# The final norm's factor row, made on TensorE instead of through DRAM, in a decoder layer's kernel

## The chip, the cores and the metric

One core of a Trainium2 chip runs the kernel. The metric is the device time in microseconds (us) of one execution. The core's engines work side by side, each through its own list of instructions in order: TensorE (PE, with its weight loads as PEld), VectorE (DVE), ScalarE (ACT), GpSimd (POOL) and SyncE (SP), which here issues the DMAs.

## The reference, cut to what matters

One layer of a hybrid decoder over 2048 prompt tokens and 8 sample tokens, 2056 in all, width 1024, float32:

```python
def _rmsnorm(x, g):
    return x * lax.rsqrt(jnp.mean(x * x, axis=-1, keepdims=True) + EPS) * g

def _layer(...):
    xr, gr, q, k, v = jnp.split(_rmsnorm(x, norm1_g) @ w_in, IN_SPLITS, axis=-1)
    rec = recurrence(conv(xr)) * gelu(gr)         # RG-LRU branch
    att = sliding_window_attention(q, k, v, sinks)
    mix = concatenate([_rmsnorm(rec, rec_norm_g), _rmsnorm(att, attn_norm_g)])
    h = x + mix @ w_out
    hn = _rmsnorm(h, norm2_g)
    return h + (silu(hn @ w_gate) * (hn @ w_up)) @ w_down     # D_FF = 2816

y = _rmsnorm(_layer(...), final_norm_g)           # the final norm
```

The change concerns the last line: each token's y (1024 values) is multiplied by one factor of that token, 1/sqrt(mean of squares + EPS), and by the gain of the feature.

## The kernel before

Activations lie transposed: features on the 128 partitions, tokens along the free dimension, so 1024 features are 8 tiles (m = 0 to 7). A factor that belongs to a token must therefore stand in every partition of a row, as a tile of 128 x tokens.

The first 600 us or so take the tokens in four blocks through the norm, the input projection, recurrence, attention and output projection; the sum h goes to DRAM (hs). Then comes the feed-forward part, in three groups of tokens (gi = 0, 1, 2) of two halves each (n = 0, 1): 2 x 344 tokens in group 0, 2 x 342 in groups 1 and 2. For each of 11 pairs p of D_FF chunks, a Strassen-like scheme makes seven products r of the gate side (ps_g) and of the up side (ps_u) in `products`, and seven of the down side (pw, for group and pair "pw1_0" is group 1, pair 0) in `down_parts`; each product is three TensorE matmuls of 342 or 344 columns, of split operands. VectorE adds every pw product into the y tiles of its group (L2175). `y_load` (L1893) fetches h into these y tiles by DMA (y<-hs, L1899), 16 tiles for each group, in buffers which the group before gives free when its y is stored.

At a group's end comes the final norm. Groups 0 and 1 go through `finish` (L2177), group 2 through `finish_last`. `finish` sums the squares of a half's eight y tiles, `rstd_cols` (L1119) sums over partitions by matmuls (st_f) and raises to the power -1/2, which gives the factors as columns: w tokens on the partitions, nt columns (w, nt = 86, 4 in group 0; 114, 3 in group 1). `dram_bcast` (L1152) turns these columns into a row: TensorE transposes them (tr_f, L1075), ScalarE copies the result out of PSUM (row_f, L1149), SyncE writes it to a row in DRAM (rows_f, L1150) and reads it back into all 128 partitions (rb_f, L1156). Then VectorE multiplies each y tile by gain and factor (L2195) and SyncE stores it (out_yT, L2196).

`row_bcast` (L1128) does the same without DRAM: for each column one matmul, with the column broadcast along its free dimension as weights and the identity as the moving operand, leaves the w factors in all partitions of a PSUM bank (bc), and ScalarE copies the bank into the row tile (L1140). The first part of the kernel uses it for its norms (bc_at, bc_rc, bc_x); `finish_last` has such products (bc_f) of its own.

The work is written as generators that run by planned due times (`Chains`); the engines' lists are then put in a fixed order by `order_engines`, from the table ORDER, which has one long string for each engine. A word such as `tr_f1_1` names a generator or a group of matmuls; `:3` means three in a row, `+2` the third of those left. SyncE, ScalarE, GpSimd and VectorE each work through their own string; a DMA's issue on SyncE waits until what it reads is written, and what stands behind it in the list waits too.

Of the kernel before, what the change touches and what calls it, by code (L numbers as in the profile page):

```python
# [155 lines left out]
pt5_0_0 op0_1_0 op0_0_0 op0_0_260:2 op0_0_0:3 op0_0_260 op0_0_0 op0_1_0 op0_0_260:2 op0_0_0 op0_0_260 op0_0_0
op0_0_260 op0_0_0 op0_1_0 op0_0_260:2 op0_1_0:5 o4_1_0:2 op0_1_260:7 o4_1_1:2 op0_1_260:14 op0_2_0 op0_1_260 op0_2_0
pt5_0_1 op0_1_260 pt5_0_1 op0_1_260 pt5_0_1 op0_2_0:3 pt5_0_1 op0_2_0:14 op0_2_260 op0_2_0 op0_2_260 op0_2_0:2
op0_2_260 op0_2_0 op0_3_0 o5_0_0 op0_2_260:2 op0_2_0 op0_2_260:2 s6_1_0 op0_2_260:2 o5_0_0 s6_1_0:2 op0_2_260:2 s6_1_0
s6_1_1:2 op0_2_260 s6_1_1 op0_2_260:2 s6_1_1 op0_2_260:10 op0_3_0:4 o5_0_1 op0_3_0:16 pt5_1_0 op0_3_0 pt5_1_0 op0_3_0  # L160
op0_3_260:2 op0_3_0 op0_3_260 pt5_1_0:2 op0_3_260 o5_0_1 op0_3_260:9 g1_2_0_0 op0_3_260 g1_2_0_0 op0_3_260:8 op0_4_0
g1_2_0_0 op0_3_260 op0_4_0:6 op0_3_260 op0_4_0:10 g1_2_1_0:2 op0_4_0:4 g1_2_1_0 op0_4_0 op0_4_260 op0_4_0 op0_4_260:3
op0_4_0 op0_4_260:17 pt5_1_1 op0_4_260:3 pt5_1_1:2 op0_5_0:2 pt5_1_1 op0_5_0:2 o5_1_0 op0_5_0 o5_1_0 op0_5_0:13
op0_5_260 op0_5_0:4 o5_1_1 op0_5_260:2 op0_5_0 op0_5_260 op0_5_0 op0_5_260:8 s7_0_0:2 op0_5_260:2 s7_0_0:2 s7_0_1:2
op0_5_260 pt6_0_0 op0_5_260 pt6_0_0 op0_5_260:3 pt6_0_0:2 op0_5_260 o5_1_1 op0_6_0 op0_5_260:3 s7_0_1:2 op0_5_260
# [796 lines left out]
def hybrid_step(tc, xT, xR, vecs, cst, gatew, win, wout, wgate, wup, wdown, kT, vC, ck, cv, sconv, sh0,  # L962
# [5 lines left out]
    with ExitStack() as ctx:  # L968
# [183 lines left out]
        def dram_bcast(cols, w, nt, name):  # L1152
            row = dp.tile([1, w * nt], F32, name=f"rows_{name}")
            rows_out(row, cols, w, nt, name)
            out = bcp.tile([P, TM], F32, tag="bc", name=f"rb_{name}")
            nc.sync.dma_start(out[:, :w * nt], row.to_broadcast([P, w * nt]))  # L1156
            return out
# [1226 lines left out]
```

## Time and profile before

| | us |
|---|---|
| runs shown | 1998.69, 1999.23, 3230.68; median 1999.23 |
| profiled execution | 1999.11 |
| its span (first to last instruction) | 1997.0 |
| TensorE busy in the span | 1971.0 |
| VectorE, ScalarE, GpSimd busy | 1560.6, 981.3, 959.8 |

The span is what the views of the profile cover; 2.1 us of the profiled time lie around it. Times in the views are counted from the start of the span. Granted TensorE clock is 0.997. Group 0's end, in the sense of this text, is about 1120 to 1165 us, group 1's about 1570 to 1615.

A row of a timeline reads: start, duration, engine, line and operation, output<-inputs, tile shapes, and in brackets the idle time ahead of it with what ended it. A row of a list of waits reads: engine and operation, what it waited for, then total, number of times and longest. Where a row of a window has four engines in a row, the first number is the window's length, the others the busy time of PE, PEld, DVE, ACT and POOL with the number of instructions.

### The profile page before, as it was taken

The numbers are of one execution on the slowest core, as the hardware profiler recorded it, in microseconds if no ns is written. First come the engines' busy times: TensorE is split into PE (matmuls) and PEld (weight loads), VectorE is DVE, ScalarE is ACT, GpSimd is POOL, SyncE is SP. The second block draws the span as 40 slices with busy tenths as digits, with TensorE's granted clock in tenths as the row PEclk, the third lists the DMA queues.
The fourth block names the chain that finished last, engine by engine and source line by source line (L and its number), as shares of the span: only waits on it lengthen the run. The fifth ranks groups of instructions, "written<-read, shape, count | busy, mean of one in ns | idle before, by whom it ended". The sixth has DMA issues, their size and how long they took to land. (4 is left out here: it accounts for less than half of the span.)

```text
span 1997.0 us, 34846 instructions
## 1 busy us (share of the span) xinstructions
PE 1971.0 (99%) x12112; PEld 1874.8 (94%) x12112; DVE 1560.6 (78%) x2894; ACT 981.3 (49%) x2032; POOL 959.8 (48%) x821
## 2 busy tenths in 40 slices
PE   8999999999999999999999999999999999999998
PEld 8988898888877999999999999999999999999998
DVE  7887986777986888888998786886668586766776
ACT  6775774664664534444446433433345433433433
POOL 5412362130233896788998754534456423322323
PEclk9999999999999999999999999999999999999999
DMA  8873586576688978655667886776558675565552
GB/s 314 287 252 138 194 300 198 183 254 210 223 283 291 335 263 268 220 215 210 246 241 279 265 289 231 234 237 210 191 191 267 228 259 199 179 211 195 180 181 103
DMA packets 218470, 461.93 MB, mean 231 GB/s; under 512 B 26230, under 2 KB 90406, under 8 KB 218278
## 3 DMA queue, kind: packets, MB, share of 16 engines
q1 hardware_dynamic: 214662, 456.69, 67.4%
q10 hardware_dynamic: 3632, 3.02, 0.4%
q8 instruction: 95, 1.56, 0.3%
q14 instruction: 81, 0.66, 0.1%
HBM read 345.51 MB, written 115.17 MB: 231 GB/s over the span
## 5 line engine op out<-in xcount | busy, mean ns | idle before, releaser
L1070 PE MATMUL ps_g<-hn,w_g 128*128 128x342 f32 (+1 forms) x2772 | 569.4, 320 | 0.3 <-DMA w_g<-split_g 0.3
L1070 PE MATMUL ps_u<-hn,w_u 128*128 128x342 f32 (+1 forms) x2772 | 559.5, 320 | 1.5 <-DMA w_u<-split_u 0.9
L1070 PEld LDWEIGHTS ps_g<-hn,w_g 128*128 128x128 f32 x2772 | 461.3, 188 | 1.2 <-ACT wd L1972 0.5
L1070 PEld LDWEIGHTS ps_u<-hn,w_u 128*128 128x128 f32 x2772 | 459.5, 188 | 3.0 <-ACT c_u L2115 1.6
L2175 DVE TENSOR_TENSOR y<-y,pw 128x342 f32<-128x342 f32 (+1 forms) x756 | 359.1, 504 | 114.7 <-PE pw L1070 108.4
L1070 PE MATMUL ip<-xn,w_in 128*128 128x512 f32 (+1 forms) x1680 | 365.2, 357 | 6.1 <-ACT xn L1105 5.7
L1070 PEld LDWEIGHTS ip<-xn,w_in 128*128 128x128 f32 x1680 | 269.6, 189 | 45.8 <-ACT xn L1105 5.7
L1070 PE MATMUL pw<-fh,wd 128*128 128x342 f32 (+1 forms) x864 | 253.4, 320 | 0.5 <-DVE y L2175 0.5
L1070 PE MATMUL pw<-t,wd 128*128 128x342 f32 (+1 forms) x972 | 243.7, 320 | 2.8 <-DVE y L2175 2.7
L1070 PE MATMUL op<-mix,w_out 128*128 128x512 f32 (+1 forms) x960 | 205.8, 355 | 0.4 <-ACT mix L1544 0.4
L1070 PEld LDWEIGHTS op<-mix,w_out 128*128 128x128 f32 x960 | 157.5, 189 | 25.3 <-ACT mix L1544 0.8
L1070 PEld LDWEIGHTS pw<-t,wd 128*128 128x128 f32 x972 | 169.9, 188 | 4.9 <-DVE y L2175 4.0
L1973 POOL TENSOR_TENSOR wd<-rd,wd 128x512 fp32r<-128x512 f32 x85 | 121.8, 1434 | 103.4 <-ACT wd L1972 99.1
L1972 ACT CAST wd<-rd 128x512 fp32r<-128x512 f32 x159 | 98.6, 621 | 130.0 <-PE ps_u L1070 39.8
L1070 PEld LDWEIGHTS pw<-fh,wd 128*128 128x128 f32 x864 | 158.6, 188 | 1.2 <-DVE y L2175 0.8
L1904 POOL TENSOR_TENSOR w_u<-ru,w_u 128x512 fp32r<-128x512 f32 x44 | 61.4, 1395 | 170.2 <-ACT w_u L1903 95.9
L1070 PE MATMUL pw<-fl,wd 128*128 128x342 f32 (+1 forms) x432 | 132.9, 320 | 0.0
L2089 DVE TENSOR_TENSOR c_u<-c_u,ps_u 128x342 f32<-128x342 f32 (+1 forms) x99 | 50.2, 508 | 101.2 <-PE ps_u L1070 93.9
L2071 POOL TENSOR_TENSOR c_u<-c_u,c_g 128x342 f32<-128x342 f32 (+1 forms) x60 | 65.4, 1090 | 124.8 <-DVE c_u L2089 115.1
L2060 DVE TENSOR_TENSOR fl<-c_u,fh 128x342 fp32r<-128x342 f32 (+1 forms) x132 | 105.4, 803 | 17.7 <-ACT fh L2059 17.0
L2059 ACT CAST fh<-c_u 128x342 fp32r<-128x342 f32 (+1 forms) x132 | 63.0, 480 | 110.6 <-POOL c_u L2071 49.3
L1070 PE MATMUL pd<-fh,w_d 128*128 128x344 f32 (+1 forms) x384 | 92.9, 320 | 0.0
(319 smaller groups left out, 3490.7 us busy)
## 6 DMA issues: line engine op xcount, KB each, us to landing
w_g<-split_g SPq DMA_DIRECT2D x88, 512.0 KB
w_u<-split_u SPq DMA_DIRECT2D x88, 512.0 KB
w_in<-split_w SPq DMA_DIRECT2D x84, 512.0 KB
rg<-in_wgate SPq DMA_DIRECT2D x110, 256.0 KB
ru<-in_wup SPq DMA_DIRECT2D x110, 256.0 KB
w_out<-split_w SPq DMA_DIRECT2D x48, 512.0 KB
split_g<-w_g SPq DMA_DIRECT2D x44, 512.0 KB
split_u<-w_u SPq DMA_DIRECT2D x44, 512.0 KB
```

The costliest lines, as they stand in the source:

```text
L1070: r = nc.tensor.matmul(*args, **kw)
L1904: lo_eng.tensor_tensor(w[:, 1, :], src, w[:, 0, :].bitcast(F32), op=ALU.subtract)
L1972: nc.scalar.copy(w[:, :, 0], v)
L1973: eng((E_DLO0, E_DLO1, E_DLO2)[gi][j]).tensor_tensor(w[:, :, 1], v, w[:, :, 0].bitcast(F32), op=ALU.subtract)
L2059: nc.scalar.copy(hi, v)
L2060: nc.vector.tensor_tensor(lo, v, hi.bitcast(F32), ALU.subtract)
L2071: (nc.vector if p == NPAIR - 1 or src is not v else eng(E_MUL[2 * h + n])).tensor_tensor(v, src, g, op=ALU.mult)
L2089: nc.vector.tensor_tensor(o, a, b, op)
L2175: nc.vector.tensor_tensor(v, v, ps, ALU.add)
```

## The change

In `finish` the factor row is made by `row_bcast` instead of `dram_bcast`. For each half of groups 0 and 1 that removes a transpose, a copy of 4 x 86 or 3 x 114, a DMA into DRAM and a broadcast DMA out of it, and adds 4 or 3 matmuls (bc_f) and a copy of 128 x 344 or 128 x 342. The multiplies and the stores are as before.

```diff
@@ -2188,7 +2190,7 @@
                 rstd_cols(acc[:, :nn], w, nt, 0, cols[:w, :nt], name, 0)
                 yield t + dt * (F_FIN[2] + F_FIN[3])
-                bc = dram_bcast(cols[:w, :nt], w, nt, name)
+                bc = row_bcast(cols[:w, :nt], w, nt, name, 0)
                 for m in range(KD):
                     yield t + dt * (F_FIN[2] + F_FIN[3])
                     v = ys[gi, n, m]
```

All five strings of ORDER are new, with the counts of all other instructions as they were. Two lines of the string of SP and of PE, before and after, from the same places (the end of group 1):

```diff
-wd2.0:2 wg2.1:4 wd2.0 wg2.2 wd2.0:2 wu2.1+4 wd2.1 f11 wu2.1 f11 wg2.2 wd2.1 wu2.1+1 wu2.1 f11+7 f10 f11+2 wu2.1 f11+4
+wd2.0:2 wu2.1+4 wd2.1 wu2.1 wg2.2 wd2.1 wu2.1+1 wu2.1 f11+5 f11+2 f11+4 f11+4 f11+1 f11+2 wu2.1 f10+2 f10+5 f10+5
```

What stands in the lists now is shown at three places. First TensorE at the end of group 0. Before, the second half's transpose (tr_f0_0) stands among the first pw products of group 1 (shape out, then the number of equal rows):

```order
L1070 MATMUL pw1_0_1_1_13737<-fl1_0_00_7464,wd1_0_0_13581 128x342
L1070 MATMUL pw1_0_5_1_13747<-fh1_0_01_7461,wd1_0_0_13581 128x342
L1070 MATMUL pw1_0_5_0_13742<-fh1_0_01_7461,wd1_0_0_13581 128x342
L1075 MATMUL tr_f0_0_13640<-cs_104,cols_f0_0_13538 4x86
L1070 MATMUL pw1_0_5_1_13747<-fl1_0_01_7465,wd1_0_0_13581 128x342
L1070 MATMUL ps_g1_1_1_13521<-hn1_1_8_13054,w_g1_1_4_13546 128x342 x4
L1070 MATMUL pw1_0_1_1_13737<-fh1_0_00_7460,wd1_0_0_13581 128x342
L1070 MATMUL pw1_0_5_0_13742<-fl1_0_01_7465,wd1_0_0_13581 128x342
L1070 MATMUL pw1_0_5_0_13742<-fh1_0_01_7461,wd1_0_0_13581 128x342
L1070 MATMUL pw1_0_1_0_13732<-fh1_0_00_7460,wd1_0_0_13581 128x342
```

Now the first of that half's four products stands near that place, and the other three behind 31 more large matmuls, ahead of the matrix product pw1_0_2:

```order
L1072 MATMUL ps_u1_1_1_13750<-hn1_0_0_12850,w_u1_1_1_13585 128x342
L1072 MATMUL ps_u1_1_1_13750<-hn1_0_1_12867,w_u1_1_1_13585 128x342 x3
L1072 MATMUL ps_u1_1_1_13750<-hn1_0_2_12887,w_u1_1_1_13585 128x342
L1072 MATMUL bc_f0_0_0_13639<-cs_104,cols_f0_0_13538 128x86
L1072 MATMUL ps_u1_1_1_13750<-hn1_0_2_12887,w_u1_1_1_13585 128x342
L1072 MATMUL bc_f0_0_0_13639<-cs_104,cols_f0_0_13538 128x86
L1072 MATMUL ps_u1_1_1_13750<-hn1_0_2_12887,w_u1_1_1_13585 128x342
L1072 MATMUL bc_f0_0_0_13639<-cs_104,cols_f0_0_13538 128x86
L1072 MATMUL ps_g1_1_5_13593<-hn1_1_6_13029,w_g1_1_3_13517 128x342
L1072 MATMUL ps_g1_1_5_13593<-hn1_1_7_13033,w_g1_1_3_13517 128x342 x3
L1072 MATMUL pw1_0_2_0_13825<-fh1_0_10_7462,wd1_0_2_13721 128x342
```

The transpose's place among the first pw rows is taken by one product; the three others have moved down to the end of the first up-side product of group 1. The lines of after are two further down (L1072 is L1070 of before).

Second, TensorE at the end of group 1, where the pw products of group 2's first pair (pw2_0) that need loaded y tiles begin. Before, they follow the last up-side product (ps_u2_1) and alternate with the gate side of the next pair (ps_g2_2):

```order
L1070 MATMUL ps_u2_1_1_18695<-hn2_1_9_18021,w_u2_1_4_18833 128x342
L1070 MATMUL ps_g2_2_1_18964<-hn2_0_0_17808,w_g2_2_1_18856 128x342
L1070 MATMUL ps_u2_1_1_18695<-hn2_1_9_18021,w_u2_1_4_18833 128x342
L1070 MATMUL ps_u2_1_1_18695<-hn2_1_10_18043,w_u2_1_4_18833 128x342 x3
L1070 MATMUL pw2_0_1_1_18680<-t2_0_7652,wd2_0_1_18624 128x342 x3
L1070 MATMUL pw2_0_1_0_18675<-t2_0_7652,wd2_0_1_18624 128x342 x3
L1070 MATMUL ps_g2_2_1_18964<-hn2_0_0_17808,w_g2_2_1_18856 128x342 x2
L1070 MATMUL ps_g2_2_1_18964<-hn2_0_1_17825,w_g2_2_1_18856 128x342
L1070 MATMUL ps_g2_2_1_18964<-hn2_0_0_17808,w_g2_2_1_18856 128x342
L1070 MATMUL ps_g2_2_1_18964<-hn2_0_1_17825,w_g2_2_1_18856 128x342 x3
L1070 MATMUL pw2_0_1_3_18811<-fh2_0_00_7640,wd2_0_3_18709 128x342
L1070 MATMUL pw2_0_1_3_18811<-fl2_0_00_7644,wd2_0_3_18709 128x342
```

Now:

```order
L1072 MATMUL ps_u2_1_5_18810<-hn2_1_6_17985,w_u2_1_3_18788 128x342
L1072 MATMUL ps_u2_1_5_18810<-hn2_1_7_17989,w_u2_1_3_18788 128x342 x3
L1072 MATMUL pw2_0_1_0_18669<-t2_0_7652,wd2_0_1_18618 128x342 x3
L1072 MATMUL pw2_0_1_3_18805<-fh2_0_00_7640,wd2_0_3_18703 128x342
L1072 MATMUL pw2_0_1_3_18805<-fl2_0_00_7644,wd2_0_3_18703 128x342
L1072 MATMUL pw2_0_1_3_18805<-fh2_0_00_7640,wd2_0_3_18703 128x342
L1072 MATMUL pw2_0_1_1_18674<-t2_0_7652,wd2_0_1_18618 128x342 x3
L1072 MATMUL pw2_0_1_0_18669<-t2_0_7652,wd2_0_2_18661 128x342
L1072 MATMUL pw2_0_1_0_18669<-t2_1_7653,wd2_0_2_18661 128x342
L1072 MATMUL pw2_0_1_0_18669<-t2_0_7652,wd2_0_2_18661 128x342
L1072 MATMUL pw2_0_1_1_18674<-t2_0_7652,wd2_0_2_18661 128x342
```

The product of weights w_u2_1_4 (10 matmuls left of it) and the gate side of the next pair stand behind these pw rows now, so pw2_0_1_0 on t2_0 comes 14 matmuls earlier and the pw rows follow one another without the other products between them. At the same end the three products of half 1 (bc_f1_1) stand some 40 large matmuls behind the old place of their transpose (tr_f1_1), those of half 0 (bc_f1_0) 7 behind theirs.

Third, SyncE at the end of group 1: stores of group 1's y (out_yT), a weight load (w_u2_1_3) and the loads of group 2's y tiles (y2<-hs). Before:

```order
L2196 DMA out_yT<-y1_5_13721 128x342
L1150 DMA rows_f1_0_18583<-row_f1_0_18586 3x114
L2196 DMA out_yT<-y1_1_13591 128x342
L1927 DMA w_u2_1_3_18794<-split_u_118 128x1024
L2196 DMA out_yT<-y1_3_13678 128x342
L1156 DMA rb_f1_0_18589<-rows_f1_0_18583 128x342
L2196 DMA out_yT<-y1_2_13636 128x342
L2196 DMA out_yT<-y1_4_13703 128x342
L1899 DMA y2_0_18524<-hs_115 128x342
L2196 DMA out_yT<-y1_3_13678 128x342
L1899 DMA y2_0_18524<-hs_115 128x342
L2196 DMA out_yT<-y1_1_13591 128x342
```

Now:

```order
L2198 DMA out_yT<-y1_3_13676 128x342
L2198 DMA out_yT<-y1_1_13591 128x342
L2198 DMA out_yT<-y1_4_13701 128x342
L2198 DMA out_yT<-y1_5_13719 128x342
L2198 DMA out_yT<-y1_1_13591 128x342
L2198 DMA out_yT<-y1_3_13676 128x342
L1929 DMA w_u2_1_3_18788<-split_u_118 128x1024
L2198 DMA out_yT<-y1_1_13591 128x342
L2198 DMA out_yT<-y1_4_13701 128x342 x2
L2198 DMA out_yT<-y1_3_13676 128x342
L1901 DMA y2_0_18522<-hs_115 128x342 x3
```

The two DMAs of the factor row are gone, the weight load stands behind six stores instead of two, and the first y load behind ten stores instead of five, with the next two directly behind it. SyncE's list is 8 DMAs shorter in all, two for each half. In the first 600 us the strings of all engines differ mostly by swaps of neighbours; near the attention's second broadcast (bc_at, copied by ScalarE at L1140) ScalarE's list has one more cast of output weights ahead of that copy.

More of the change, by code (lines that the diff above doesn't have):

```diff
@@ new lines @@
+w0_4_5_0 g0_5_5 w0_4_2_0 w0_4_1_0 g0_5_5:3 w0_4_5_0:2 w0_4_5_1:2 g0_5_5:5 w0_4_6_1 g0_5_7:2 w0_4_6_0 g0_5_7:2
+w0_4_2_0:2 g0_5_7:2 g0_5_3 g0_5_7:5 g0_5_3 g0_5_7 w0_4_6_1 g0_5_3 w0_4_6_0:2 g0_5_3 w0_4_6_1 w0_4_3_0:2 g0_5_3:3
+w0_4_3_0 g0_5_3:5 w0_4_3_1:3 g0_5_4:12 w0_4_1_3 w0_4_7_0:3 w0_4_7_1:3 u0_5_1 u0_5_2 w0_4_2_1:3 w0_4_1_2:3 u0_5_1
+w0_4_4_0:3 w0_4_4_1:2 w0_4_1_3 w0_4_4_1 w0_4_1_3 u0_5_1:5 w0_4_5_2:2 u0_5_1:3 w0_4_5_2 u0_5_1 w0_4_6_2:2 u0_5_1
+w0_4_6_2 u0_5_5 w0_4_5_3:3 u0_5_5 w0_4_6_3 u0_5_2 w0_4_6_3:2 u0_5_2:2 w0_4_3_2:3 u0_5_6:5 w0_4_3_3:3 u0_5_6:2
@@ new lines @@
+w2_2_1_0 w2_2_1_1 u2_2_4 w2_2_1_0 w2_2_1_1 u2_2_4:8 g2_3_6 u2_2_4 g2_3_6:3 g2_3_2 u2_2_4 g2_3_2 g2_3_6:3 g2_3_2:7
+g2_3_6 g2_3_2:3 g2_3_6:4 w2_2_5_0 w2_2_5_1 g2_3_5:2 w2_2_5_0 g2_3_5 w2_2_5_0 w2_2_5_1:2 g2_3_5:3 w2_2_6_0 g2_3_5:6
+w2_2_6_0 w2_2_6_1 w2_2_6_0 g2_3_7:3 w2_2_6_1 g2_3_7 w2_2_6_1 w2_2_3_0 g2_3_7:2 w2_2_3_0 g2_3_7 w2_2_3_0 g2_3_7
+w2_2_3_1:3 g2_3_7:2 w2_2_2_0 g2_3_7:2 w2_2_2_0 w2_2_7_0:2 w2_2_7_1 w2_2_2_0 w2_2_7_1:2 g2_3_3 w2_2_7_0 g2_3_3:5
+w2_2_2_1 g2_3_3:3 w2_2_2_1 g2_3_3:3 w2_2_1_2:2 w2_2_2_1 w2_2_1_3:2 g2_3_4:3 w2_2_1_2 w2_2_4_0 g2_3_4:2 w2_2_1_3
@@ new lines @@
+g2_6_3:2 w2_5_2_1:2 g2_6_3 w2_5_2_1 g2_6_3:4 w2_5_1_3 g2_6_3 w2_5_1_2 g2_6_3 w2_5_1_2 w2_5_4_0 w2_5_1_2 w2_5_1_3:2
+w2_5_4_0:2 g2_6_4:3 w2_5_4_1 g2_6_4 w2_5_4_1 g2_6_4:2 w2_5_4_1 w2_5_6_2 g2_6_4:5 u2_6_1 w2_5_6_2 g2_6_4 w2_5_6_2
+u2_6_1 w2_5_6_3 u2_6_1 w2_5_5_2:2 w2_5_6_3 u2_6_1 w2_5_6_3 w2_5_5_2 w2_5_5_3 u2_6_1:4 w2_5_5_3 u2_6_1 w2_5_5_3
+u2_6_1:2 u2_6_2 u2_6_1 u2_6_2:2 w2_5_7_2 u2_6_2:2 w2_5_7_2 w2_5_7_3:2 w2_5_7_2 u2_6_2 w2_5_7_3 w2_5_3_2 u2_6_2
+w2_5_3_2:2 w2_5_3_3 u2_6_2 w2_5_3_3 u2_6_2:4 w2_5_2_2 w2_5_3_3 w2_5_2_2 u2_6_6:3 w2_5_2_2 u2_6_6:2 w2_5_4_3 u2_6_6
@@ new lines @@
+w2_9_4_2:2 w2_9_4_3:2 d2_10_0_1:2 u2_10_4 d2_10_1_1 d2_10_0_1:3 d2_10_1_1:5 d2_10_2_1 d2_10_0_1 d2_10_2_1 d2_10_3_1
+d2_10_2_1:2 d2_10_4_1 d2_10_2_1:2 d2_10_3_1:4 d2_10_4_1 d2_10_3_1 d2_10_5_1 d2_10_4_1:4 d2_10_5_1 d2_10_6_1
+d2_10_5_1:4 d2_10_6_1:5 d2_10_7_1:6 d2_10_0_0:5 d2_10_1_0:4 st_f2_1:6 d2_10_0_0 d2_10_1_0:2 d2_10_2_0:3 d2_10_3_0:2
+bc_f2_1:3 d2_10_2_0:3 d2_10_3_0:4 d2_10_4_0:4 d2_10_5_0 d2_10_4_0:2 d2_10_5_0:3 d2_10_6_0 d2_10_5_0:2 d2_10_6_0:5
+d2_10_7_0:6 w_st_f2_0:9 w_bc_f2_0:3 st_f2_0:6 bc_f2_0:3
@@ L619 @@
+d1.0+3 pu1.1+1 d1.0:2 d1.0+1 d1.0:2 pu1.1+1 pu1.1 d1.0 d1.1 d1.0 pu1.1 d1.1 pg1.2 pu1.1+1 d1.1:2 pu1.1 wd1.1 d1.1
+d1.1+5 pu1.1 d1.1 pu1.1 d1.1:2 wd1.1 d1.1 pg1.2 d1.1 wu1.2 d1.1 d1.1+2 wd1.1+1 d1.1+2 pg1.2 d1.1+1 d1.1 wd1.1 mix2+4
 d1.1+2 d1.1+2 d1.1:2 d1.1+2 d1.1+2 d1.1 pu1.2 d1.1:2 wg1.3 d1.1+1 d1.1+1 pu1.2 d1.1 wd1.2+1 pu1.2:4 pu1.2+1 d1.2:2
@@ L852 @@
+wg2.9:2 wd2.8 wg2.9 wu2.9 wg2.9 wd2.8 wg2.10 wu2.9+4 wg2.10 wd2.9:3 wu2.9 wd2.9:2 wu2.9:3 wg2.10+4 wu2.10 wd2.9+1
+wg2.10:2 wd2.9 wg2.10 wu2.10 wg2.10 wd2.9 wd2.10 wu2.10+4 wd2.10:2 wu2.10:3 wd2.10 wu2.10 f21 f21+1 f21+1 f21+1 f21
+f21+1 f21:2 f20:4
 """,
```

1389 lines of the change are left out of this document (683 added, 706 removed).

## The prediction

> **What bounds the kernel now.** I read the page first, for the engines' shares and the chain of waits.
>
> ```profile
> span 1997.0 us, 34846 instructions
> ## 1 busy us (share of the span) xinstructions
> PE 1971.0 (99%) x12112; PEld 1874.8 (94%) x12112; DVE 1560.6 (78%) x2894; ACT 981.3 (49%) x2032; POOL 959.8 (48%) x821
> ...
> PE 41%; DMA 1%; DVE 1%; POOL 0%; issue 0%; ACT 0%; SPq 0%; DVEq 0%; POOLq 0%; ACTq 0%
> ```
>
> TensorE is busy for 1971.0 of 1997.0 us, and no other engine has more than 1% of the chain. What is not TensorE work is 26 us in all, beginning and end included. So an edit can win only TensorE instructions or TensorE waits. The second view is therefore the list of what TensorE waits for, over the whole span:
>
> ```profile
> PE ip L1070 <- ACT xn L1105: 5.7, 1, 5.7
> PE pw L1070 <- DVE y L2175: 3.3, 5, 1.2
> PE bc_at L1070 <- ACT rb_at L1140: 2.4, 1, 2.4
> PE s L1070 <- DVE mx L1639: 1.1, 1, 1.1
> PE ps_u L1070 <- DMA w_u<-split_u: 0.9, 1, 0.9
> ```
>
> The first is the start of the kernel, the third and fourth lie in the attention stage. The second and the fifth can belong to the ends of groups 0 and 1, which this change touches; the busy time of these stretches (span, then PE, PEld and so on) says how much is lost there:
>
> ```profile
> 1140.00:1160.00 20.00, 17.18 (x99) 15.14 (x98) 18.21 (x36) 5.30 (x11) 6.15 (x7) 1.00 0.94 302
> 1160.00:1570.00 410.00, 410.00 (x2613) 409.79 (x2612) 297.75 (x531) 168.16 (x347) 206.26 (x177) 1.00 0.69 229
> 1570.00:1600.00 30.00, 28.20 (x178) 26.92 (x176) 19.61 (x33) 11.82 (x26) 12.54 (x11) 1.00 0.74 239
> ```
>
> 2.8 us go at the first end, 1.8 at the second, nothing in the 410 us between. TensorE's waits in 1140 to 1170, and then in 1570 to 1610, are:
>
> ```profile
> PE pw L1070 <- DVE y L2175: 1.9, 3, 0.7
> PE ps_u L1070 <- DMA w_u<-split_u: 0.9, 1, 0.9
> ```
>
> ```profile
> PE pw L1070 <- DVE y L2175: 1.4, 2, 1.2
> PE ps_u L1070 <- ACT c_u L2117: 0.4, 1, 0.4
> ```
>
> So 2.8 and 1.8 us again. The first pw products of the next group wait for adds into y tiles. Those tiles are loaded only when the old group's y has been multiplied by the factor row and stored. The factor row is what the change makes in another way. With every one of these waits gone the kernel would be 4.6 us shorter, 0.2% of its time; the change cannot do more at these two places.
>
> **The change, part by part.** The profiled execution took 1999.11 us: its span of 1997.0 and 2.1 around it. The median of the runs shown is 1999.23, so a sum made against the profiled execution stands 0.1 us from the median.
>
> *TensorE work.* Four transposes go (tr_f, one per half), 14 broadcast products come (4 for each half of group 0, 3 for each of group 1). Rows for both, the attention's broadcast products of 104 columns and one transpose's share of the chain:
>
> ```profile
> 214.55 1.03 PE L1070 MATMUL bc_at<-cs,atcols 104*128 104x104 f32 x8
> ```
>
> ```profile
> 1586.44 0.10 PE tr_f L1075
> 1586.54 2.07 PE ps_u L1070 x13
> ```
>
> Eight products in 1.03 us are 0.129 each, 14 are 1.8. A transpose holds the path for 0.10, four are 0.4. Sum +1.4 us, all of it on the path, since TensorE sets the time. Bounds: each product as cheap as the transpose (0.10) gives 1.4 − 0.4 = +1.0; each as dear as a product of 342 columns (2.07 / 13 = 0.16) gives 2.2 − 0.4 = +1.8. The widths, 86 and 114, stand on either side of the row's 104, so I keep +1.4. [...]
>
> *The path from the norm's columns to the factor row, end of group 0.* SyncE's two instructions of the first half, then VectorE's work with the factor row (the bracket is its idle time before):
>
> ```profile
> 1131.42 0.27 SPq L1150 DMA_DIRECT2D rows_f<-row_f  x1
> 1133.18 0.33 SPq L1156 DMA_DIRECT2D rb_f<-rows_f  x1
> ```
>
> ```profile
> 1130.90 0.24 PE L1075 MATMUL tr_f<-cs,cols_f 86*4 86x86 f32 x1
> ...
> 1134.31 0.24 PE L1075 MATMUL tr_f<-cs,cols_f 86*4 86x86 f32 x1
> ...
> 1136.86 3.68 DVE L2195 SCALAR_TENSOR_TENSOR y<-y,vec,rb_f 128x344 f32<-128x344 f32 x5 [0.94 <-DMA rb_f<-rows_f]
> ...
> 1138.77 0.32 SPq L1156 DMA_DIRECT2D rb_f<-rows_f  x1
> ...
> 1143.02 2.03 DVE L2195 SCALAR_TENSOR_TENSOR y<-y,vec,rb_f 128x344 f32<-128x344 f32 x4
> ```
>
> From transpose to first multiply are 5.96 us. In the new order the first half's products stand 10 to 13 big products behind the transpose's old place: 13 × 0.16 + 4 × 0.129 = 2.6 us, then a copy of 344 columns, for which the nearest row is this:
>
> ```profile
> 219.39 0.49 ACT L1140 COPY rb_at<-bc_at 128x416 f32<-128x416 f32 x1
> ```
>
> So the factors are there 2.6 + 0.5 = 3.1 us after 1130.90, at 1134.0 instead of 1136.86. The second half's products are split: one stands about where the transpose was, three stand 31 big products later, directly ahead of the first product of the third matrix pair, at about 1134.3 + 8 × 0.16 + 31 × 0.16 + 1.0 for all eight products = 1141.5; with the copy 1142. Before, the row was issued at 1138.77 and, at the first half's 3.7 us from issue to use, there at about 1142.4. So the first half gains 2.8 us at most and 0.9 at least (VectorE idled only 0.94 for it), the second 0.4. SyncE loses four of its instructions here and the waits between them, ahead of the very weight load for which TensorE then waits 0.9. What was late by the sum of 1.9 + 0.9 moves forward by 1 to 2.8. I take −2.0, inside these; bounds −2.8 (all gone) and +1.0, since the order also puts the first of those pw products some 21 places (3.4 us) earlier, which can give a wait back.
>
> *End of group 1.* The same rows there:
>
> ```profile
> 1583.15 2.03 DVE L2195 SCALAR_TENSOR_TENSOR y<-y,vec,rb_f 128x342 f32<-128x342 f32 x4 [0.77 <-DMA rb_f<-rows_f]
> ...
> 1593.63 0.51 DVE L2089 TENSOR_TENSOR c_u<-c_u,ps_u 128x342 f32<-128x342 f32 x1 [3.70 <-ACT c_u L2117]
> 1594.07 4.71 DVE L2195 SCALAR_TENSOR_TENSOR y<-y,vec,rb_f 128x342 f32<-128x342 f32 x6
> ```
>
> ```profile
> L2195 DVE SCALAR_TENSOR_TENSOR y<-y,vec,rb_f x32: 560/566/1607, 1136.9 to 1600.6; 128x344 f32<-128x344 f32 x16, 128x342 f32<-128x342 f32 x16
> L1520 DVE SCALAR_TENSOR_TENSOR rrec<-gt,rrec x16: 676/686/5470, 100.8 to 567.2; 128x512 f32<-128x512 f32 x12, 128x520 f32<-128x520 f32 x4
> ```
>
> The first half's products are placed some 40 big products behind the old transpose; counted back from the second transpose at 1586.3 they end near 1585, and with the copy the multiplies start at 1585.7 instead of 1583.15: 2.5 us later. The second half's stand 7 behind the old transpose: ready at 1586.3 + 7 × 0.16 + 0.4 + 0.5 = 1588.3 instead of 1594.07, where VectorE had stood idle for 3.70. Sixteen multiplies of 0.57 and two adds of 0.51 from 1585.7 on end at about 1595.8, against 1599.7 (1599.12 and 0.57). The first y add of the next group comes behind them, so it is some 3 us earlier than its present place. The first pw product that needs it is placed 14 products (2.2 us) earlier. So the wait of 1.4 shrinks by 0.8 to 0.6; the 0.4 behind ScalarE's copy of c_u stays, as the products on both sides of it keep their order. But the pw products now stand in one run of about 38 with nothing between them, where the other products lay between before. I take −0.5; bounds −1.8 and +4 (the second rival).
>
> *All other new positions.* Every engine's order is renumbered, mostly by swaps of neighbours from 0 to 600 us. The work is the same and TensorE is nearly gapless there but for the waits listed. I take 0. Downward at most the 2.4 of the bc_at wait and a little of the others, say −3; upward the third rival's +4.8.
>
> Sum: +1.4 − 2.0 − 0.5 + 0 = −1.1 on 1999.1, so **1998.0 us**.
>
> **Rivals.**
>
> *First: both ends lose all their waits* (2.8 and 1.8). For it: the waits follow from lateness of y, and VectorE's multiplies end 3 us sooner. Against: the pw products were placed earlier by about as much. 1999.1 + 1.4 − 4.6 = 1995.9.
>
> *Second, the slower side: the run of pw products at the end of group 1 starves.* SyncE's list there now has ten stores and the weight load ahead of the first y load; the tenth store needs the tenth multiply, 1585.7 + 10 × 0.57 = 1591.4 at best. At the chain's price for such a load,
>
> ```profile
> 1151.74 2.73 DMA y<-hs
> ```
>
> the tile lands at 1594.1 and VectorE, if free, adds at once; that is in time for 1596. But two or three multiplies that take the 1.6 us of the row's maximum make stores, loads and adds late together, by 1.0 us each, and in a dense run each add is waited for. The dense pw products behind the end of group 0 lost 1.9 us by the row above. It decides from about 1593 on as the time of the first y load. Price: the 1.4 stays, 2 or 3 more come and the weight load behind six stores brings up to 1: +4, so 1999.1 + 1.4 − 2.0 + 4 = 2002.5.
>
> *Third: a long VectorE block in the first 600 us lands elsewhere.* One rrec step took 5470 ns where the median is 686, and that block reached TensorE as the 2.4 us wait of bc_at. The new order has a cast ahead of the copy waited for, and VectorE, GpSimd and ScalarE swap neighbours at many places there. [...] A second such block, 5.47 − 0.69 = 4.8 us, all of it on the path, gives 1998.0 + 4.8 = 2002.8; none where there is one now gives 1998.0 − 2.4 = 1995.6.
>
> *Fourth: the DRAM path was hidden, and nothing comes back.* VectorE waited for it 0.94 and 0.77 us only, and stores and loads are paced by SyncE. Then only the work is left: 1999.1 + 1.4 = 2000.5.
>
> **How the numbers follow.** Chances: my forecast 0.45, first rival 0.17, second 0.14, third 0.12 (two thirds of it upward), fourth 0.12. The range goes down to the first rival with the −3 of the other positions, 1995.9 − 3 = 1992.9, rounded down to 1992; upward the second and the third together would give 2002.5 + 4.8 = 2007.3, of which I leave out the last us, since both at once are rare: 2006. Two per cent is 40 us, about what tells this kernel from no change; the waits and the added work are 5 us and the whole of TensorE's idle time is 26. Faster by over 2% is impossible by this account and slower would need a stall not seen anywhere in it: 0.01, 0.97 and 0.02.
>
> **What would show it.** In the profile after: 14 more bc_f products and no tr_f, at 0.10 to 0.16 us each on the chain; the first multiplies near 1134 and 1585.7, the second half's of group 1 near 1588; VectorE's 3.7 us of idleness before 1593 gone; the pw waits for y and the w_u wait behind group 0 under 1 us in sum, those behind group 1 near 1. The prediction is wrong if pw waits behind the end of group 1 exceed 3 us, if the attention stage shows a new wait of over 2 us, or if TensorE's busy time changes by more than 2 us.

## The result, and the profile after

The changed kernel takes 2006.5 us (median of six runs, 2003.7 to 2010.14) against 1999.38 before: ratio 1.0038, 95% interval 1.0028 to 1.0048, so 7 us slower. The profiled execution took 2003.7, which is the fastest of the six; its span is 2001.9 us, 4.9 longer than before. The page of the changed kernel:

```profile
span 2001.9 us, 34871 instructions
...
PE 1976.3 (99%) x12136; PEld 1879.5 (94%) x12136; DVE 1559.2 (78%) x2894; ACT 979.8 (49%) x2032; POOL 960.1 (48%) x821
```

TensorE has 24 records more than before, not the 10 that I counted (14 products less 4 transposes). Its waits over the span (total, times, longest):

```profile
PE ip L1072 <- ACT xn L1107: 5.5, 1, 5.5
PE ps_g L1072 <- DMA w_g<-split_g: 2.6, 1, 2.6
PE pw L1072 <- DVE y L2177: 1.4, 2, 0.7
```

The waits of pw for y have shrunk from 3.3 to 1.4 us, the one for w_u behind group 0 is gone, and a wait of 2.6 us for gate weights w_g is new. It lies behind the end of group 1; the list of 1570 to 1650 us has

```profile
PE ps_g L1072 <- DMA w_g<-split_g: 2.6, 1, 2.6
PE pw L1072 <- DVE y L2177: 0.7, 1, 0.7
PE ps_u L1072 <- ACT c_u L2119: 0.4, 1, 0.4
```

Where the time went shows best if one instruction is set against itself. For each kind of VectorE and ScalarE instruction I took the n-th of one trace and the n-th of the other, and the median difference of their starts in slices of 50 us: how far the changed kernel is behind (+) or ahead (-) of the kernel before at that place. It is 4.0 us ahead at 450 us, level at 1050, 1.2 ahead at 1175, 0.2 ahead at 1550 and 4.7 behind at 1650, and stays so. The two ends of groups therefore count -1.3 and +4.9; the rest comes to +1.3 by these slices (0.0 up to 1050, +1.1 from 1175 to 1550, where the list of waits has 0.7 us for w_u weights, +0.2 after 1650). The table gives the same for the experiments below.

| trace | up to 1050 us | end of group 0 (1050 to 1175) | end of group 1 (1550 to 1650) |
|---|---|---|---|
| after | 0.0 | -1.3 | +4.9 |
| after again (e10) | -0.2 | -0.9 | +7.3 |
| old orders, edit alone (e1) | -0.3 | +2.2 | +1.0 |
| old order in the last part (e2) | +3.2 | -0.6 | +0.7 |
| new order in the last part (e3) | +0.8 | +0.8 | +5.9 |
| w_g2_2_7 earlier (e4) | -2.4 | -1.3 | +6.0 |
| w_g2_2_6 earlier (e5) | +1.4 | -1.3 | +0.9 |
| edit and new order in group 0 only (e6) | -1.4 | -1.0 | +0.8 |
| wait filled (e7) | +2.3 | -1.6 | +5.2 |
| before, w_g2_2_6 later (e8) | +0.4 | -0.3 | +7.9 |
| new orders, DRAM path (e9) | -1.7 | +6.8 | +12.7 |

The first column differs by some 5 us between traces of the same orders there (after, e2, e4, e5, e7, e9 and e10 all have the new ones), so a single trace says nothing on that part. Two things that come and go make most of this spread. One is a stretch at half the TensorE clock near 600 us: 6.83 us long in e2 and e7, 3.41 in after and e5, absent in e4, e9 and e10. The other is a wait of pw for y near 1058 us, described under e6, which e2, e5, e6, e9 and e10 have and which costs them 1.3 us each (the slice at 1050 us, with which this column ends, contains it). The third column is the story.

**The end of group 1 in detail.** Ahead of the wait, at it, and behind it (window's length, then busy PE, PEld, DVE, ACT, POOL, granted clock, DMA share, GB/s):

```profile
1600.00:1613.00 13.00, 13.00 (x81) 12.57 (x81) 9.49 (x21) 2.69 (x5) 1.86 (x2) 1.00 0.90 282
1613.60:1616.50 2.90, 0.29 (x2) 0.00 (x2) 1.52 (x4) 0.57 (x2) 0.08 (x1) 1.00 0.97 351
1616.50:1620.00 3.50, 3.47 (x13) 3.50 (x14) 0.41 (x1) 0.00 (x0) 0.00 (x0) 0.53 0.95 348
```

The third row is what I had not looked for: TensorE is busy all the time, but does 13 matmuls in 3.5 us where 22 would fit, at a granted clock of 0.53 (in the trace's own record of the clock it is 0.50 from 1616.72 to 1620.13, 3.41 us, and 1.00 on both sides). The wait is paid twice: 2.6 us of standing, and 13 x (0.285 - 0.157) = 1.7 us of slow running (0.285 us from start to start of its matmuls in that stretch, 0.157 as the median of the trace). The product waited for uses w_g2_2_6. SyncE's instructions there, of the changed kernel:

```profile
1606.49 0.39 SPq L2037 DMA_DIRECT2D rd<-sums_d  x1
1606.92 0.43 SPq L2032 DMA_DIRECT2D rd<-in_wdown  x1
1607.39 0.43 SPq L2033 DMA_DIRECT2D rd<-in_wdown  x1
1607.93 1.74 SPq L1929 DMA_DIRECT2D w_g<-split_g  x1
1609.71 0.43 SPq L1917 DMA_DIRECT2D rg<-in_wgate  x1
1610.19 0.43 SPq L1901 DMA_DIRECT2D y<-hs  x1
1610.71 0.38 SPq L2037 DMA_DIRECT2D rd<-sums_d  x1
1611.13 0.44 SPq L1929 DMA_DIRECT2D w_g<-split_g  x1
```

and of the kernel before:

```profile
1607.85 0.80 SPq L1927 DMA_DIRECT2D w_g<-split_g  x2
1608.70 0.43 SPq L2035 DMA_DIRECT2D rd<-sums_d  x1
1609.17 0.43 SPq L2030 DMA_DIRECT2D rd<-in_wdown  x1
```

The kernel before has a small wait for this load already, and its load takes, by the chain of waits:

```profile
PE ps_g L1070 <- DMA w_g<-split_g: 0.3, 1, 0.3
...
1607.85 4.88 DMA w_g<-split_g
```

By the lists, the first w_g of before is w_g2_2_6 and the second w_g2_2_7; now w_g2_2_7 comes fourth, and w_g2_2_6 eighth, at 1611.13. Most places cost SyncE some 0.43 us, one 1.74, and the load then takes

```profile
1611.13 5.26 DMA w_g<-split_g
```

by the chain of waits. So it lands at 1616.4; TensorE wanted it at 1613.9.

Sum at this end: products 6 x 0.22 less two transposes +1.1, the w_g wait +2.6 less the 0.3 of before, the slow clock +1.7, the waits for y 0.7 instead of 1.4, -0.7. Together +4.4 of the 4.9; the rest I have not placed.

**The products.** In the changed kernel, at the end of group 0, they alternate with large products:

```profile
1132.42 0.35 PE L1072 MATMUL bc_f<-cs,cols_f 86*128 86x86 f32 x2
1132.56 0.40 PE L1072 MATMUL ps_g<-hn,w_g 128*128 128x342 f32 x1
1132.80 0.35 PE L1072 MATMUL bc_f<-cs,cols_f 86*128 86x86 f32 x2
```

One product is two records (x2), and one period of product and large product is 0.38 us, of which the large one is 0.157 (the median of its starts over the trace). So a product costs 0.22 (group 1's, 114 wide, start 0.38 us apart from 1583.76 on, which gives the same), 14 cost 3.1, less 0.4 for the transposes: +2.7.

### The profile page after: what moved, and what is told of

The parts are those of the page before. It is cut to its first block, busy times and chain, and to the rows that moved or that the text cites. A ratio compares the mean times of both kernels' runs of the same rounds, so it can differ in the third digit from the quotient of the medians.

```text
span 2001.9 us, 34871 instructions
## 1 busy us (share of the span) xinstructions
PE 1976.3 (99%) x12136; PEld 1879.5 (94%) x12136; DVE 1559.2 (78%) x2894; ACT 979.8 (49%) x2032; POOL 960.1 (48%) x821
## 4 chain that ended last, share of the span: by engine, by line
PE 92%; DMA 3%; DVE 3%; POOL 1%; issue 1%; ACT 1%; SPq 0%; DVEq 0%; ACTq 0%; POOLq 0%
PE ps_g L1072 21%; PE ps_u L1072 21%; PE pw L1072 17%; PE ip L1072 15%; PE op L1072 7%; PE pd L1072 4%; PE s L1072 1%; PE o L1072 1%; PE pt L1077 1%; PE g L1072 1%; DMA out_yT<-y 1%; DMA m<-mixed 1%; DMA y<-hs 0%; DVE sc L1652 0%; DMA w_u<-split_u 0%
## 5 line engine op out<-in xcount | busy, mean ns | idle before, releaser
L1072 PE MATMUL ps_g<-hn,w_g 128*128 128x342 f32 (+1 forms) x2772 | 571.7, 320 | 2.6 <-DMA w_g<-split_g 2.6
L1072 PE MATMUL ps_u<-hn,w_u 128*128 128x342 f32 (+1 forms) x2772 | 560.8, 320 | 1.3 <-DMA w_u<-split_u 0.7
L1072 PEld LDWEIGHTS ps_g<-hn,w_g 128*128 128x128 f32 x2772 | 462.2, 189 | 3.5 <-issue 2.9
L1072 PEld LDWEIGHTS ps_u<-hn,w_u 128*128 128x128 f32 x2772 | 459.7, 188 | 2.9 <-DMA w_u<-split_u 1.3
L1072 PE MATMUL ip<-xn,w_in 128*128 128x512 f32 (+1 forms) x1680 | 365.2, 357 | 6.3 <-ACT xn L1107 5.5
L1072 PEld LDWEIGHTS ip<-xn,w_in 128*128 128x128 f32 x1680 | 269.6, 189 | 46.5 <-ACT xn L1107 5.5
L1072 PE MATMUL pw<-fh,wd 128*128 128x342 f32 (+1 forms) x864 | 254.9, 321 | 0.1
L1072 PE MATMUL pw<-t,wd 128*128 128x342 f32 (+1 forms) x972 | 243.3, 320 | 1.7 <-DVE y L2177 1.4
L1072 PE MATMUL op<-mix,w_out 128*128 128x512 f32 (+1 forms) x960 | 206.6, 356 | 0.3 <-ACT mix L1107 0.2
L1072 PEld LDWEIGHTS op<-mix,w_out 128*128 128x128 f32 x960 | 157.5, 189 | 25.8 <-DVE mix L1108 0.5
L1072 PEld LDWEIGHTS pw<-t,wd 128*128 128x128 f32 x972 | 169.8, 188 | 3.6 <-DVE y L2177 2.8
L1072 PEld LDWEIGHTS pw<-fh,wd 128*128 128x128 f32 x864 | 159.1, 189 | 1.5 <-DVE y L2177 0.8
L1072 PE MATMUL pw<-fl,wd 128*128 128x342 f32 (+1 forms) x432 | 133.2, 320 | 0.0
L1905 ACT CAST w_g<-rg 128x512 fp32r<-128x512 f32 x99 | 61.0, 621 | 69.5 <-PE pw L1072 23.7
```

The source lines that it names most:

```text
L1072: r = nc.tensor.matmul(*args, **kw)
L1905: nc.scalar.copy(w[:, 0, :], src)
```

## Experiments

Each kernel was timed in turn with the kernel before, except e10, which is a single run. Orders are strings that can be cut where old and new agree on every engine; three parts were put together, cut at about 870 us and 1350 us.

**e1, e2, e3: which part of the change loses the time.** e1 keeps every old string and changes only what the edit needs:

```diff
-tr_f0_1      (PE; likewise tr_f0_0, tr_f1_1, tr_f1_0)
+bc_f0_1_0:4  (3 in group 1; SyncE's two entries of each half left out)
```

> The edit alone: broadcast products and copy instead of the way through DRAM, but every engine in the order of the kernel before. The products of a half stand in a row where its transpose stood, the two DMAs of each half are left out. Theory (the loss is the new order at the end of group 1): the 14 products are 28 matmul records in the trace, chain price about 0.21 us each product, so +2.5 after the transposes, and the factor rows come earlier, which gives back 1 to 2 of the waits for y: 2000 to 2001.5. Rival (the loss is the edit itself, on TensorE and in PSUM): 2003 or more.

Measured: 2000.67 against 1999.95, ratio 1.0011 (1.0001 to 1.0020), so the edit itself is some 2 of the 7 us by the ratio, 0.7 by the medians, and not the rest. But the waits did not shrink either; TensorE's from 1140 to 1170 and from 1570 to 1620 in e1:

```profile
PE pw L1063 <- DVE y L2168: 1.9, 3, 0.7
PE ps_u L1063 <- DVE w_u L1897: 0.9, 1, 0.9
```

```profile
PE pw L1063 <- DVE y L2168: 1.4, 2, 1.2
PE ps_u L1063 <- ACT c_u L2110: 0.4, 1, 0.4
```

These are the numbers of before, to the tenth (the wait for w_u weights is put down to another releaser). The factor rows are ready sooner (VectorE no longer waits for them, where it waited 0.94 and 0.77 us before), but VectorE's old list has the multiplies behind other work, so they start no sooner for it:

```profile
1137.23 4.15 DVE L2188 SCALAR_TENSOR_TENSOR y<-y,vec,rb_f 128x344 f32<-128x344 f32 x5
...
1597.15 4.70 DVE L2188 SCALAR_TENSOR_TENSOR y<-y,vec,rb_f 128x342 f32<-128x342 f32 x6
```

(1136.86 and 1594.07 before; this trace is 2 to 3 us behind at the second place.) In the old order the way through DRAM was hidden, and the edit alone costs its products. That is what my fourth rival said (2000.5).

e2 is the changed kernel with the old order, edit included, in the last part; e3 has the new order in the last part only.

```diff
 e2: new up to 870 us, new up to 1350 us,
-    new behind it
+    old behind it
 e3: old up to 870 us, old up to 1350 us, new behind it
```

> The changed kernel with the new orders up to the middle of group 1's feed-forward part (about 1350 us) and the old order, with the edit in it, from there on. Theory (the loss is the new order at the end of group 1, where the trace of after falls back by 4.9 us): 2006.5 - 4.9 + 1 = 2002.5 or less. Rival (the loss is spread over the earlier orders, in small waits for weights that come and go): 2005 to 2007.

> The complement: old orders with the edit up to the middle of group 1's feed-forward part, the new order from there on. Theory (end of group 1): e1 plus 3.5 to 4.9, so 2004 to 2006, with a TensorE wait of some 2.6 us for w_g behind the end of group 1. Rival (spread over the earlier orders): within 1 us of e1.

Measured: e2 2002.18, ratio 1.0009 (0.9998 to 1.0019); e3 2005.86, ratio 1.0035 (1.0023 to 1.0047), with a wait of 3.0 us for w_g. The new order from 1350 us on carries the loss. e2 also shows a gain at the end of group 0 with its products paid, as do all traces with the new order there and the edit.

**e4: a miss.** I meant to put w_g2_2_6 back ahead of the loads into rd buffers and took the wrong entry: the load moved is its neighbour w_g2_2_7.

```diff
+L1929 DMA w_g2_2_7
 L2037 DMA rd2_1_2
 L2032 DMA rd2_1_3
 L2033 DMA rd2_1_3
-L1929 DMA w_g2_2_7
 ...
 L1929 DMA w_g2_2_6
```

> The changed kernel with one place in SyncE's list changed: the weight load w_g2_2_6 goes back ahead of the three loads into rd buffers, where the kernel before has it. Theory (that load stands behind issues which wait for GpSimd's wd, so TensorE waits 2.6 us for it): the wait goes, 2006.5 - 2.6 = 2003.9. Rival (the load is late for want of DMA capacity, not by its place): 2006 to 2007 and the wait stays above 1.5 us.

Measured: 2006.62, ratio 1.0030 (1.0018 to 1.0042), the wait for w_g 2.7. The text on record names the wrong load, so neither side is decided by it; it shows that moving the other load forward does not help.

**e5 and e8: the place of w_g2_2_6.** e5 is the changed kernel with that load ahead of the three rd loads; e8 is the kernel before, DRAM path and all, with that load where the changed kernel has it.

```diff
 e5 (changed kernel)              e8 (kernel before)
+w_g2_2_6                        -w_g2_2_6
 rd2_1_2                          w_g2_2_7
 rd2_1_3 (two DMAs)               rd2_1_2
 w_g2_2_7                         rd2_1_3 (two DMAs)
 rg, y2_4, rd2_1_4                rg, y2_4, rd2_1_4
-w_g2_2_6                        +w_g2_2_6
```

> The changed kernel with the weight load w_g2_2_6 back ahead of the loads into rd buffers in SyncE's list (e4 had moved w_g2_2_7, its neighbour, by a wrong index, and the wait stayed). In the trace of after, that load is issued at 1611.13 and lands 5.26 us later; TensorE stands 2.6 us for it, and then runs 13 matmuls at a granted clock of 0.53, 1.6 us more. Theory (place of w_g2_2_6 in SyncE's list): wait and slow clock go, 4 us less: 2002 to 2003. Rival (the DMAs behind the end of group 1 are late as a whole): less than 1.5 us gained, another wait for weights takes its place.

> The kernel before, factor rows through DRAM, with one move in SyncE's list: the load w_g2_2_6 goes behind the loads into rd buffers, where the changed kernel has it. Theory (place of that load alone makes the loss): a TensorE wait of 2 to 3 us for w_g and a slow stretch behind it, 3 to 4.5 us slower than before: 2003 to 2004.5. Rival (it needs the rest of the new order or the products): under 1.5 us slower.

Measured: e5 2002.27, ratio 1.0015 (1.0005 to 1.0024). TensorE's waits in 1570 to 1640 are now these, with none for w_g:

```profile
PE ps_u L1066 <- ACT wd L1968: 0.9, 1, 0.9
PE pw L1066 <- DVE y L2171: 0.8, 1, 0.8
```

e8 2006.96, ratio 1.0038 (1.0025 to 1.0051), which is more than the 3 to 4.5 us that I expected. One entry of SyncE's list, moved seven issues down in the old kernel, makes it as slow as the whole change does; moved up in the new kernel, it gives back about 4 us. The 3 us that e5 still loses are about the price of the products (2.7); that is a sum and not a test. In e8 the wait is longer than in after; TensorE's wait (1600 to 1630), the load in the chain, and three windows:

```profile
PE ps_g L1064 <- DMA w_g<-split_g: 6.5, 1, 6.5
```

```profile
1611.59 7.71 DMA w_g<-split_g
```

```profile
1613.00:1616.50 3.50, 0.00 (x0) 0.00 (x0) 1.91 (x4) 1.57 (x3) 0.52 (x1) 0.91 0.98 352
1617.00:1619.00 2.00, 0.00 (x0) 0.00 (x0) 0.00 (x0) 0.00 (x0) 0.00 (x0) 0.50 0.08 30
1619.40:1622.50 3.10, 3.06 (x11) 3.10 (x12) 0.00 (x0) 0.00 (x0) 0.00 (x0) 0.50 0.00 0
```

It is issued at about the same time as in after (1611.59 against 1611.13) and takes 7.7 us instead of 5.3. In the first half of the wait the DMA engines are full (0.98); from 1617 to 1619 their mean share is 0.08, about one of the page's 16 engines (16 x 0.08 = 1.3). From that I estimate that the load waited for the last engine or two; no view shows which, or why.

**e7: standing and running slowly, taken apart.** Twenty matmuls of no use go ahead of the first product with w_g2_2_6, so TensorE works through most of the wait.

```diff
+w_pw2_0_2_3:20
 g2_2_6:7
```

> The changed kernel with 20 matmuls of 256 columns without use put into TensorE's list just ahead of the first product that needs w_g2_2_6, into a bank that is written anew afterwards; at 0.118 us each they take 2.4 us of the wait. Theory (a wait of almost 3 us has the granted clock fall to about half for the next 3.5 us): the wait for the weights stays in sum, the slow stretch goes, 1.6 us less than the changed kernel: 2004.5 to 2005. Rival (the slow stretch has another cause, such as the load on DMA): the granted clock behind the wait stays at about 0.5 and the time does not fall.

Measured: 2004.32, ratio 1.0023 (1.0013 to 1.0033), 2.2 us less than the changed kernel (against its own runs of before 4.3 us slower instead of 7.1; the two intervals overlap a little). Its TensorE rows, and the windows at and behind the wait:

```profile
1616.37 2.64 PE L1066 MATMUL pw<-ones 128*128 128x256 f32 x20
1619.67 0.55 PE L1066 MATMUL ps_g<-hn,w_g 128*128 128x342 f32 x2 [0.67 <-DMA w_g<-split_g]
```

```profile
1616.30:1619.00 2.70, 2.70 (x22) 2.45 (x20) 1.45 (x4) 0.50 (x2) 0.01 (x1) 1.00 1.05 392
1619.60:1623.00 3.40, 3.33 (x21) 3.36 (x22) 1.48 (x4) 0.00 (x0) 0.00 (x0) 1.00 1.00 341
```

With a wait of about the same length (2.6 filled, 0.67 on top), 21 matmuls run in 3.4 us at a granted clock of 1.00, though DMA share is 1.00 as well. So the slow stretch (0.53 behind the unfilled wait in after, at a DMA share of 0.95) comes from TensorE's standing, not from the load on DMA. The time is less well shown than the clock: in this one trace the end of group 1 counts +5.2, no less than in after, as two waits for w_u (1.6 us together) have come there. In after, a wait of 2.6 us was enough for 3.41 us at half the clock; which waits had it behind them is taken up under e10.

**e6: the part that gains, alone.** Broadcast products in group 0 with the new order around its end; everything before 870 us and behind 1350 us as before, with the DRAM path in group 1.

```diff
-bc = row_bcast(cols[:w, :nt], w, nt, name, 0)
+bc = dram_bcast(cols[:w, :nt], w, nt, name) if gi else row_bcast(cols[:w, :nt], w, nt, name, 0)
```

> Broadcast products for group 0 alone with the new order around its end; the first part and everything behind the middle of group 1's feed-forward part, factor rows through DRAM included, as in the kernel before. Theory (the new order gains at the end of group 0: -1.2 us in the trace of after, products paid): 1998.5 to 1999.5 against 1999.95 before. Rival (the gain of one trace is chance): 2000 to 2002.

Measured: 2000.05 against 2000.04, ratio 0.9996 (0.9987 to 1.0006). The 1 us at the end of group 0 is in its trace, but the time cannot be told from before and is not the 1998.5 to 1999.5 that I expected. The new order also costs something ahead of that end. TensorE's waits in 1040 to 1110 of e6 are

```profile
PE pw L1063 <- DVE y L2168: 1.0, 1, 1.0
```

and the trace falls back by 1.3 us there. Five of the eight traces with the new order at this place have this wait, none of the four with the old. So what the end of group 0 gains is about taken back 70 us earlier when this wait comes. e6 is the best of the variants, and no gain that I can claim.

**e9: the new orders without the edit.** The way through DRAM again, the new lists otherwise, w_g2_2_6 first.

```diff
-bc_f0_1_0  (PE, first product of the half; the others left out)
+tr_f0_1
+rows_f     (SyncE, two entries ahead of the half's first store)
+rb_f       (SyncE, directly ahead of it)
```

> The edit undone and the new orders kept: factor rows through DRAM, the transpose where the new order has a half's first product, the write of the row two places and its broadcast read directly ahead of the half's first store in SyncE's list, and w_g2_2_6 first as in e5. Theory (the new positions at the end of group 0 gain only because the factor row comes earlier): the waits for y behind group 0, 0.7 us in e5, go up by 2 us or more, group 1's second half likewise, and the 2.7 us of the products are saved: 2002 to 2005. Rival (the positions gain by themselves, the way of the factor row is hidden): waits as in e5, products saved: 1999.5 to 2000.5.

Measured: 2018.7, ratio 1.0096 (1.0075 to 1.0116), far over what either side expected. TensorE's waits from 1100 to 1200:

```profile
PE ps_g L1064 <- DVE c_g L2083: 3.3, 1, 3.3
PE ps_u L1064 <- DVE c_g L2083: 2.6, 1, 2.6
```

and two of VectorE's multiplies there:

```profile
1136.19 0.58 DVE L2189 SCALAR_TENSOR_TENSOR y<-y,vec,rb_f 128x344 f32<-128x344 f32 x1 [6.44 <-DMA rb_f<-rows_f]
...
1149.97 0.58 DVE L2189 SCALAR_TENSOR_TENSOR y<-y,vec,rb_f 128x344 f32<-128x344 f32 x1 [8.83 <-DMA rb_f<-rows_f]
```

The new lists have VectorE's multiplies at the place where the broadcast products deliver. With the row late, VectorE stands 6 to 9 us at its first multiply, and behind it in its list are the c_g steps for which TensorE waits. So the edit is worth much to the new orders, nothing to the old ones. Part of the +19 may be my placing of the two DMAs.

**e10: the same kernel, a second trace, and when a wait brings the slow clock.**

> The changed kernel once more, for a second trace of the same list. Theory (the load w_g2_2_6 is late by an amount that changes from run to run): a TensorE wait of 2 to 7 us for w_g behind the end of group 1, and the time above or below 2003.7 by about what that wait differs from 2.6. Rival (the spread of this kernel's times has another origin): the wait is again 2.6 within 0.3 us while the time differs by more than 1 us.

Measured: 2006.42, 2.7 us over the first trace's run. The wait for w_g is 3.8, and the two windows at and behind it are

```profile
1613.70:1617.70 4.00, 0.24 (x2) 0.02 (x1) 1.47 (x4) 0.52 (x2) 0.04 (x1) 0.81 0.98 358
1617.70:1622.70 5.00, 4.99 (x18) 5.00 (x19) 1.76 (x5) 0.00 (x0) 0.00 (x0) 0.50 0.71 267
```

The wait is 1.2 us longer and the slow stretch 5.0 instead of 3.5 us; this end costs 7.3 instead of 4.9. (By the record of the clock, half speed lasts here from 1616.21, within the wait, to 1623.03.) That 2.4 is most of the 2.7. The text on record allowed only the 1.2 us of the longer wait; it left the slow stretch out. So this wait and its slow stretch account for most of the difference between these two runs (the half-clock stretch near 600 us that only after has, 1.7 us as half of its 3.41, and the wait near 1058 us that only e10 has, 1.3 us, nearly cancel); for the other runs I have no trace.

The length of a wait alone did not decide whether the clock fell. In e9, TensorE stands for 2.26 us up to 1596.45 and for 3.56 us up to 1605.58; the windows are behind the first wait, in the second, and behind it:

```profile
1596.90:1600.30 3.40, 3.40 (x14) 3.40 (x14) 2.98 (x6) 0.00 (x0) 0.00 (x0) 0.50 0.57 196
1602.10:1605.50 3.40, 0.00 (x0) 0.00 (x0) 0.00 (x0) 1.33 (x3) 0.00 (x0) 1.00 0.73 205
1605.60:1607.60 2.00, 2.00 (x12) 1.81 (x12) 1.69 (x4) 0.00 (x0) 0.00 (x0) 1.00 0.12 43
```

The shorter wait is followed by half the clock, the longer one is not. In each of the twelve traces' records of the clock, the half-clock stretches (that of the kernel's end apart, 8.34 us in after) are 3.41 or 6.83 us long, and within a trace they begin a whole number of steps of 3.413 us apart (in after the one at 1616.72 lies 298 steps behind the one at 599.55, in e9 the one at 1596.89 lies 135 behind the one at 1136.09). I laid these steps over TensorE's waits, by the records of its matmuls. The nine steps in which it stood 1.89 us or more at full clock were all followed by half the clock (before: 1.89 us within the step up to 221.45; after: 2.64 us within the step up to 1616.72); the 3.56 us in e9 fall into two steps, 1.71 and 1.86 us, and were not. So in these traces a wait of 2 to 3.6 us was dear or not by where it fell. This fits all of them but for the first 8 us of the kernel (the record of the clock begins only at 9.0 us in after and 9.8 in before) and the stretch near 600 us, which I have not explained: in after it comes behind 1.11 us of standing within the step, and before stands 1.13 us in a step there at full clock.

## Why the prediction was wrong

I forecast 1998.0 with a range to 2006; it is 2006.5. By its own steps:

- **End of group 1, taken at -0.5 without products and with a bound of +4: wrong, +4.9 and +7.3 in two traces, or +3.8 and +6.2 without the 1.1 for the products.** This is the step that failed. I followed SyncE's new list through the stores and w_u2_1_3 to the first y loads and stopped there. Some 28 entries further on, the load w_g2_2_6 had gone from the first to the eighth place behind the last of that run of y loads, while the kernel before already showed 0.3 us of waiting for it. e5 and e8 show that this one place makes the loss, by a wait for w_g of 2.6 and 3.8 us in the two traces and the half clock behind it. What I did weigh came out nearly as worked out: first half's multiplies at 1585.41 (1585.7 forecast), the second half's at 1589.37 (1588.3), and the wait for y 0.7 (0.6).

- **The second rival, 2002.5, had the sign and the place but not the mechanism.** I let the y loads come late and the dense pw run starve. The first y load was issued at 1592.76, ahead of the 1593 from which it would decide, and pw lost only 0.7. "The weight load behind six stores" was the wrong one: w_u is not among the waits at this end in the trace of after.

- **The price of a wait.** I took each TensorE wait at its length. Here a wait of 2.6 us cost 4.3. The slow clock was in the trace of before as well, behind the attention wait of 2.35 us (the first window); it came 1.5 us after the wait had ended:

```profile
217.50:219.90 2.40, 0.07 (x1) 0.00 (x0) 1.90 (x5) 1.02 (x2) 0.00 (x0) 1.00 0.80 305
219.90:221.40 1.50, 1.47 (x7) 1.27 (x8) 1.00 (x3) 0.78 (x2) 0.00 (x0) 1.00 0.16 66
221.50:224.80 3.30, 3.30 (x11) 2.72 (x10) 2.55 (x5) 2.71 (x5) 1.55 (x3) 0.50 0.00 0
```

- **TensorE work, taken at +1.4 (bounds +1.0 to +1.8): mis-sized, +2.7.** The eight records of my row are four products, two records each; counted so, the row gives 0.26 per product instead of 0.129. The count of the group, 34 records for 17 columns, said so. TensorE's busy time, which I had named as a sign if it changed by more than 2 us, rose by 5.3.

- **End of group 0, taken at -2.0 without products: right, if a little small** (-1.3 and -0.9 in the table, -2.9 and -2.5 without the 1.6 for the products). The waits there went from 2.8 to 0.7 us:

```profile
PE pw L1072 <- DVE y L2177: 0.7, 1, 0.7
```

The first multiply is at 1134.05 (1134 forecast). With 1.6 for the products the waits alone would make -0.5; the table has -1.3 and -0.9, so short pauses that the list of waits does not name went too. The wait near 1058 us, which the new order brings in five of eight traces, I had not seen. e1 and e9 add what I had not seen: neither the edit nor the order gains this alone.

- **All other new positions, taken at 0: not contradicted.** Up to 1050 us the seven traces with the new orders lie between -2.4 and +3.2, the four others' between -1.4 and +0.8. The third rival's wait for bc_at is gone in all seven traces with the new orders there, while four of the five with the old ones have it with 2.3 or 2.4 us and e1 with 0.4; so its better half came true. The times at 1050 us do not show the gain clearly, as the half-clock stretch near 600 us costs 1.7 or 3.4 us (half of its 3.41 or 6.83) in some traces of either order. What made the one rrec step 5.47 us long, no run shows.

- **The range** ended at 2006. I had added the second and the third rival, 2007.3, and left out the last us. Neither of the two struck; that 2006.5 lies near this end is luck, and the mechanism that did strike was not among the terms.

## What to carry to other kernels

When an order is regenerated, follow every queue past the edit until old and new lists agree again, and check each load against the time at which its first user wants it; here a load with a wait of 0.3 us lost seven places, and the wait became 2.6. Price a TensorE wait with the slow clock that may stand behind it: 1.7 us behind the 2.6 in after, and by half of its 6.83 us an estimated 3.4 in e10; matmuls of no use in the wait kept the clock at 1.00 in e7. An earlier result is worth something only if the list of the engine that uses it has the user early too (in e1 the first multiply is at 1137.23, against 1136.86 before).

## What the runs showed of the hardware that I had not expected

- TensorE's granted clock was 1.00 or 0.50, the latter for 3.41 us (after, behind a wait of 2.6 us) or 6.83 us (e10 and e8, beginning within waits of 3.8 and 6.5 us). A step of 3.413 us with 1.89 us or more of standing (before) was followed by it, one with up to 1.86 (e9) was not, the kernel's first 8 us and the stretch near 600 us apart. Behind a wait filled with matmuls (e7, 0.67 left) it stayed at 1.00.
- One broadcast product of float32 columns (86 or 114 wide) is two records in the trace and takes 0.22 us between large products.
- The load of 512 KB took 4.9, 5.3 and 7.7 us from issue to landing in three traces (before, after, e8), the longest with a DMA share of 0.08 in its last 2 us.
